# The ConvGLU up-projection of a streaming encoder layer as seven block products instead of eight, from activations that are not yet normalised, with the down products in between

## The chip, the cores and the metric

The kernel runs on one core of a Trainium2 chip. The metric is the device time of one launch in microseconds (us), lower is better. TensorE is called PE here, and its weight loads PEld; VectorE is DVE, ScalarE is ACT, GpSimd is POOL, and SP issues most of the loads.

## The reference

One layer of a hybrid encoder for 640 tokens: 512 of one new stream, and 16 of each of eight running streams. Only the second half of the layer is changed:

```python
h = x + mix @ p['w_o']
hn = rms_norm(h, p['g_ffn'])
up = hn @ p['w_up']                       # 1024 -> 2 x 2816
a, b = jnp.split(up, [D_FF], axis=-1)
c, new_conv = causal_depthwise_conv(a, conv_hist, p['conv_w'], p['conv_b'])   # width 3, by channel
out = h + (jax.nn.gelu(c) * b) @ p['w_down']
```

A final RMS norm follows. All of it is float32.

## The kernel before

**Layout.** Activations lie with features on the 128 partitions and the 640 tokens along the columns: 8 tiles of the model's features, 22 tiles of each half of the up-projection. A matmul takes 128 x 128 weights and 320 tokens (HT). Operands are rounded to a type of fewer bits (F32R), so every operand is two parts, high and low, and every product is three matmuls: high by high, high by low, low by high (mm3, below). A *segment* is the six matmuls of one block of weights over both halves of the tokens; most of the work is written out segment by segment.

```python
120  def mm3(ps, u, b, x, start, stop):
121      hi, lo = (z[:, b * 128:b * 128 + 128] for z in pairs[u])
124      for h in range(2):
125          mm(bank(ps, h)[:, :HT], hi, xh[:, hs[h]], start, False)
126      for h in range(2):
127          mm(bank(ps, h)[:, :HT], hi, xl[:, hs[h]], False, False)
128      for h in range(2):
129          mm(bank(ps, h)[:, :HT], lo, xh[:, hs[h]], False, stop)
155  def slot(u, segs):
156      later(0, lambda: load(u + 3))
157      later(0, lambda: split_hi(u + 1))
158      later(2, lambda: split_lo(u + 1))
```

**Order.** Each engine works through its own instructions strictly in the order in which the program issues them; a tile framework adds the waits. The program keeps a clock of segments: `later(n, fn)` puts a step n segments ahead, and `tick()` issues what is due before each segment's matmuls. Weights come in units of eight blocks (128 x 1024, 512 KB): SP loads unit u + 3 while u is multiplied, ACT rounds unit u + 1 to its high part (L107), and DVE subtracts to get the low part (L112).

**The changed part.** The output projection (eight units, o_evac at L1125) adds the residual, makes the two parts of each normalised tile (times the norm's weights, L170 and L176; the token's 1/rms is applied later, as RS), and sums the squares. Then, for each of the 22 tiles f: one unit gives the gate half (a_evac, L1169 to L1171: PSUM times RS), one the value half (b_evac, L1195); between them DVE runs the convolution (L1179, L1181 twice), ACT the GELU (L1185, L1186), DVE the product (L1198), and ACT and DVE its two parts (L168, L174). POOL copies history and new history (L1168, L1177, L1178). After eight tiles come eight units of down products (L1226 adds each result to h), after eight more the same, and the last six tiles end in the final stage: down products over tokens 0 to 383, then over 384 to 639, with squares (L1249), norm and output (L1265). PARTS = (8, 8, 6) says so.

Of the kernel before, what the change touches and what calls it, by code (L numbers as in the profile page):

```python
# [37 lines left out]
def body(nc, tc, d, ctx):  # L38
# [37 lines left out]
    rst = const.tile([128, 8], F32, name="rst")  # L76
# [19 lines left out]
    res_pool = [None]  # L96

    def split_hi(u):
        if u < N_UNITS:
            if res_pool[0] is not None and u < N_UNITS - 2:  # L100
                hi = res_pool[0].tile([128, 1024], F32R, tag="rh", name=nm("rh"))
                lo = res_pool[0].tile([128, 1024], F32R, tag="rl", name=nm("rl"))
            else:
                hi = wp.tile([128, 1024], F32R, tag="wh", name=nm("wh"))
                lo = wp.tile([128, 1024], F32R, tag="wl", name=nm("wl"))
            pairs[u] = (hi, lo)
            A.activation(hi, raws[u], AF.Copy)  # L107

    def split_lo(u):
        if u < N_UNITS:  # L110
            hi, lo = pairs[u]
            V.tensor_tensor(lo, raws[u], hi.bitcast(F32), op=OP.subtract)  # L112
# [18 lines left out]
    # ---------------------------------------------------------------- events, by segment  # L131
# [8 lines left out]
    def tick():  # L140
        """Start of a segment: what is due, then a piece of the side work."""
# [11 lines left out]
    # one slot per unit: the next unit is split and a later one loaded while this one is multiplied  # L153
# [8 lines left out]
    def split_into(dst, src, scale, d_hi, d_lo):  # L162
        """dst = [hi, lo] of src (times a column), later"""
# [59 lines left out]
    # ---------------------------------------------------------------- side work: S5  # L223
# [7 lines left out]
    def scan_order(t):  # L231
        """(chunk, j) of the prompt and (n, i, j) of the samples in a tile of (j, c) columns"""
# [21 lines left out]
    def paced(ops, budget):  # L254
        """Run (cost, fn) pairs, pausing when the vector engine's share of a segment is used up."""
# [9 lines left out]
    def s5():  # L265
# [62 lines left out]
        # th modulo 2 pi, then sine and 1 - cosine of a quarter of it, doubled twice  # L328
# [33 lines left out]
        # powers 0..8 of lambda-bar  # L362
# [43 lines left out]
        # (lambda-bar - 1) / lambda  # L406
# [17 lines left out]
        def cmul(o_re, o_im, a, b, t, cost):  # L424
            """(o_re, o_im) = a * b, elementwise"""
# [21 lines left out]
        # chunk inputs of the states; the within-chunk response  # L447
# [58 lines left out]
        # C by (part, state) on partitions, [re; im] and [im; re], groups in the order (q, g2, g); in this  # L506
        # order PF of all groups, on both halves of the partitions
# [50 lines left out]
        def stack(q):  # L558
            """The states of eight groups, parts and states on partitions"""
# [66 lines left out]
        # outputs of the chunks  # L626
# [13 lines left out]
    # ---------------------------------------------------------------- side work: attention  # L640
# [36 lines left out]
    def attention():  # L677
# [69 lines left out]
        def prompt_pv(t0, hp, t, ms):  # L747
            # the two heads of a tile in turn: their products lie in two column tiles of the array
# [155 lines left out]
    # ---------------------------------------------------------------- start: norm and the first two units  # L904
# [4 lines left out]
    A.activation(rst, ones[:, 0:8], AF.Sqrt)  # L909
# [91 lines left out]
    # ---------------------------------------------------------------- input projection  # L1001
# [56 lines left out]
    # ---------------------------------------------------------------- GLU, attention's projection, mix  # L1058
# [56 lines left out]
    # ---------------------------------------------------------------- output projection, residual, norm  # L1115
    h_, hn = [], []
    acc2 = mp.tile([128, T], F32, name="acc2", bufs=1)
    xr = {}

    def load_x(i):  # L1120
        if i < 8:
            xr[i] = mp.tile([128, T], F32, tag="xr", name=nm("xr"))
            S.dma_start(xr[i], d["x"][i])

    def o_evac(i, ps):  # L1125
        h = ht()
        V.tensor_tensor(two(h), ps[:, :, :HT], two(xr[i]), op=OP.add)
        load_x(i + 2)
        p = pair()
        split_into(p, h, vcol(C_GF + i), 0, 1)  # L1130
        hn.append(p)
        h_.append(h)
        later(2, lambda: square_h(mp, acc2, h, i == 0))
        if i == 7:
            st = stat_steps(mp, [acc2], RS, 0, 5, ("sS", "sT", "sX"))
            for j, f in enumerate(st):
                later(6 + j, f)
# [3 lines left out]
    later(7, lambda: None)  # L1141

    def o_proj(i):
        ps = bigps()
        slot(U_O + i, [lambda k=k: mm3(ps, U_O + i, k, mixh[k], k == 0, k == 7) for k in range(8)])
        later(0, lambda: o_evac(i, ps))

    for i in range(8):
        o_proj(i)

    # ---------------------------------------------------------------- ConvGLU
    fctx = ExitStack()
# [9 lines left out]
    state = {}  # L1162

    def a_evac(f, ps):
        a = fp[0].tile([128, NA], F32, tag="a", name=nm("a"))
        asm = a[:, 514:NA].rearrange("p (n s) -> p n s", n=NS)
        G.memset(a[:, 0:2], 0.0)  # L1167
        G.tensor_copy(asm[:, :, 0:2], hist[:, f])  # L1168
        V.tensor_tensor(a[:, 2:322], ps[:, 0, :HT], RS[:, 0:320], op=OP.mult)  # L1169
        V.tensor_tensor(a[:, 322:514], ps[:, 1, 0:192], RS[:, 320:512], op=OP.mult)  # L1170
        V.tensor_tensor(asm[:, :, 2:18], ps[:, 1, 192:320].rearrange("p (n i) -> p n i", n=NS),  # L1171
                        RS[:, 512:640].rearrange("p (n i) -> p n i", n=NS), op=OP.mult)
        c = fp[0].tile([128, L], F32, tag="c", name=nm("c"))
# [263 lines left out]
```

## Time and profile before

| | us |
|---|---|
| device time, median of 3 runs (lowest, highest) | 969.23 (967.4, 973.29) |
| span of the profiled execution | 967.0 |
| busy PE, DVE, ACT, POOL in it | 949.5, 543.6, 305.8, 78.2 |

The span runs from the first to the last instruction of the profiled execution; the device time of the runs has besides it what lies before and behind, some 2 us against the median. Busy time counts overlapping matmuls once. DVE is busy in 56% of the span, ACT in 32%, POOL in 8%.

### The profile page before, as it was taken

The page shows a single profiled execution, that of the slowest core. Times are in us where ns is not written, and L with a number is a line of the kernel's source. Part 1 is how long each engine was busy: PE and PEld are TensorE (multiplying, and loading weights), DVE is VectorE, ACT ScalarE, POOL GpSimd, SP SyncE. Part 2 cuts the span into 40 slices and gives each one's busy share as a digit, 9 for nine tenths or more (in the row PEclk, how much of TensorE's full clock was granted, in tenths as well). Part 3 has the DMA queues.
Part 4 walks back from the last instruction along what each step waited for, and adds up shares of the span by engine and source line. Part 5 has one row for each costly group of instructions (what it writes and reads, how often), then busy time and mean ns, then how long its engine had stood idle before and what let it go on. Part 6 is the DMA issues. An engine that isn't in the chain of part 4 may idle for free.

```text
span 967.0 us, 16339 instructions
## 1 busy us (share of the span) xinstructions
PE 949.5 (98%) x6788; PEld 906.3 (94%) x6788; DVE 543.6 (56%) x1033; ACT 305.8 (32%) x497; POOL 78.2 (8%) x157
## 2 busy tenths in 40 slices
PE   8999999999999999999999999999999999999996
PEld 8978999977677899999999999999999999999996
DVE  6884995666565445484555555324555533455545
ACT  7153113434343454433432222111222211122231
POOL 0121303100000000000001101000110100011000
PEclk9999999999999999999999999999999999999998
DMA  6743429764764432223323222222212222222203
GB/s 224 198 150 102 131 83 123 244 191 157 212 184 175 107 101 75 79 93 107 128 66 88 66 87 66 88 66 68 87 66 88 67 87 66 72 82 69 88 28 108
DMA packets 48889, 105.60 MB, mean 109 GB/s; under 512 B 19440, under 2 KB 22704, under 8 KB 48816
## 3 DMA queue, kind: packets, MB, share of 16 engines
q1 hardware_dynamic: 45104, 95.90, 33.0%
q0 software_dynamic: 2848, 7.88, 2.7%
q8 instruction: 53, 0.87, 0.4%
q10 hardware_dynamic: 864, 0.78, 0.2%
q14 instruction: 20, 0.16, 0.1%
HBM read 91.49 MB, written 8.21 MB: 103 GB/s over the span
## 4 chain that ended last, share of the span: by engine, by line
PE 94%; DMA 2%; DVE 2%; ACT 1%; issue 1%; SPq 0%; DVEq 0%; ACTq 0%
PE pb L115 83%; PE sS L115 3%; PE sX L115 2%; DMA qs<-qs 1%; PE sP L115 1%; PE sT L738 1%; PE sX L814 1%; DMA wr<-in_w 1%; PE sS L786 1%; PE sT L802 0%; PE sT L468 0%; DVE ql L668 0%; PE sT L115 0%; DVE h L1265 0%; PE sX L817 0%
## 5 line engine op out<-in xcount | busy, mean ns | idle before, releaser
L115 PE MATMUL pb<-h,wh 128*128 128x320 f32 (+1 forms) x3488 | 665.9, 312 | 1.9 <-ACT h L944 1.0
L115 PEld LDWEIGHTS pb<-h,wh 128*128 128x128 f32 x3488 | 546.1, 188 | 10.5 <-issue 5.2
L115 PE MATMUL pb<-h,wl 128*128 128x320 f32 (+1 forms) x1744 | 400.3, 309 | 0.0
L115 PEld LDWEIGHTS pb<-h,wl 128*128 128x128 f32 x1744 | 292.4, 188 | 0.0
L107 ACT ACTIVATE wh<-wr 128x1024 fp32r<-128x1024 f32 x112 | 118.5, 1058 | 325.2 <-PE pb L115 241.6
L112 DVE TENSOR_TENSOR wl<-wr,wh 128x1024 fp32r<-128x1024 f32 x112 | 136.6, 1220 | 36.7 <-ACT wh L107 36.5
L1226 DVE TENSOR_TENSOR h<-pb,h 128x640 f32<-128x640 f32 x16 | 13.2, 824 | 76.7 <-PE pb L115 76.7
L1169 DVE TENSOR_TENSOR a<-pb,RS 128x320 f32<-128x320 f32 x22 | 10.8, 492 | 77.1 <-PE pb L115 74.9
L1195 DVE TENSOR_TENSOR b<-pb,RS 128x640 f32<-128x640 f32 x22 | 18.1, 825 | 55.4 <-PE pb L115 55.4
L693 ACT ACTIVATE sb<-sb,mx 128x128 f32<-128x128 f32 (+4 forms) x40 | 24.2, 605 | 70.7 <-DVE mx L692 47.2
L1181 DVE SCALAR_TENSOR_TENSOR c<-a,vec,c 128x656 f32<-128x656 f32 x44 | 39.7, 902 | 1.6
L1185 ACT ACTIVATE g<-c 128x512 f32<-128x512 f32 x22 | 13.9, 632 | 83.3 <-DVE c L1181 83.3
L1177 POOL COPY oc<-a 128x2 f32<-128x2 f32 x22 | 4.1, 187 | 371.8 <-DVE a L1170 371.8
L725 DVE CUSTOM_DVE_ANT_0 sb<-sS,pb 128x128 f32<-128x128 f32 (+3 forms) x32 | 15.7, 490 | 24.0 <-PE sS L115 23.8
L115 PE MATMUL pb<-h,rh 128*128 128x384 f32 (+1 forms) x128 | 28.2, 312 | 0.1
L1167 POOL MEMSET a<- 128x2 f32 x22 | 2.1, 96 | 310.7 <-DVE rst L207 310.7
L1046 DVE TENSOR_TENSOR h<-pb,RS 128x640 f32<-128x640 f32 x16 | 13.2, 824 | 19.4 <-PE pb L115 9.9
L1178 POOL COPY oc<-a 128x16 f32<-128x16 f32 x22 | 23.9, 1085 | 0.2
L168 ACT ACTIVATE h<-g 128x640 fp32r<-128x640 f32 x22 | 16.3, 739 | 22.8 <-DVE g L1198 22.8
L115 PEld LDWEIGHTS pb<-h,rh 128*128 128x128 f32 x128 | 21.4, 188 | 0.4 <-DVE h L1240 0.4
L115 PE MATMUL pb<-wh,h 128*128 128x512 f32 x64 | 21.7, 398 | 0.0
L115 PE MATMUL pb<-h,rl 128*128 128x384 f32 (+1 forms) x64 | 19.8, 309 | 0.0
(225 smaller groups left out, 845.0 us busy)
## 6 DMA issues: line engine op xcount, KB each, us to landing
wr<-in_w SPq DMA_DIRECT2D x116, 512.0 KB, 3.6
kc<-in_kc SPq DMA_DIRECT2D x16, 512.0 KB, 6.4
vc<-in_vc SPq DMA_DIRECT2D x16, 512.0 KB, 6.0
xr<-in_x SPq DMA_DIRECT2D x8, 320.0 KB, 2.9
x<-in_x SPq DMA_DIRECT2D x7, 320.0 KB, 6.3
pb<-in_pbias SPq DMA_DIRECT2D x8, 256.0 KB, 6.8
o_y<-h SPq DMA_DIRECT2D x8, 192.0 KB, 1.9
us<-h POOLq DMA_DIRECT2D x4, 320.0 KB, 5.6
```

What stands on the lines that cost most here:

```text
L107: A.activation(hi, raws[u], AF.Copy)
L112: V.tensor_tensor(lo, raws[u], hi.bitcast(F32), op=OP.subtract)
L115: PE.matmul(ps, lhs, rhs, start=start, stop=stop)
L168: A.activation(hi, src, AF.Copy)
L693: A.activation(sb[:, :w], sb[:, :w], AF.Exp, bias=mx[:, 2:3], accum_out=mx[:, 3:4])
L725: V.tensor_tensor_reduce(sb[:, :w], sc[:, :w], pbs[h][:, 512 - w:512], 1.0, -3.0e38, op0=OP.add, op1=OP.max, accum_out=mx[:, 1:2])
L1046: V.tensor_tensor(two(o), ps[:, :, :HT], two(RS), op=OP.mult)
L1178: G.tensor_copy(oc[0][:, f, 2:18].rearrange("p (n s) -> p n s", n=NS), asm[:, :, 16:18])
L1181: V.scalar_tensor_tensor(c, a[:, j:L + j], vcol(C_CW + 3 * f + j), c, op0=OP.mult, op1=OP.add)
L1185: A.activation(g[:, 0:512], c[:, 0:512], AF.Gelu_apprx_tanh)
L1195: V.tensor_tensor(two(b), ps[:, :, :HT], two(RS), op=OP.mult)
L1226: later(0, lambda: V.tensor_tensor(two(h_[i]), ps[:, :, :HT], two(h_[i]), op=OP.add))
```

## The change

The gate and the value block of a tile are taken as one product of 2 x 2 blocks: two blocks of outputs, two halves of the 1024 inner features (k 0 to 3 and 4 to 7), two halves of the tokens. It is computed with seven block products (Strassen's scheme in Winograd's form), each of four k by three matmuls:

```diff
-PARTS = (8, 8, 6)
+PARTS = (2, 4, 4, 4, 4, 4)
...
+    def parts_far(pool, tags, key, src, width):
+        hi, lo = (pool.tile([128, width], F32R, tag=t, name=nm(t)) for t in tags)
+        n = src.shape[-1]
+        A.activation(lo[:, 0:n], src, AF.Copy, scale=-1.0)
+        A.activation(hi[:, 0:n], src, AF.Copy)
+        G.dma_start(lo[:, 0:n], src, accum_op=OP.add)
...
+    def parts_near(pool, tags, key, src, width):
...
+        A.activation(hi[:, 0:n], src, AF.Copy)
+        V.tensor_tensor(lo[:, 0:n], src, hi[:, 0:n].bitcast(F32), op=OP.subtract)
...
+    def weight_sums(f):
...
+        V.tensor_tensor(s1, a21, a22, op=OP.add)
+        V.tensor_tensor(s2, s1, a11, op=OP.add)
+        V.tensor_tensor(s3, a11, a21, op=OP.add)
+        V.tensor_tensor(s4, s2, a12, op=OP.add)
...
+    PRODUCTS = (("A11", "B11", "sS"), ("s1", "t1", "sP"), ("s2", "t2", "sT"), ("A12", "B21", "sS"),
+                ("s3", "t3", "sX"), ("A22", "t4", "sT"), ("s4", "B22", "sP"))
...
+    def gate(f):
+
         G.tensor_copy(asm[:, :, 0:2], hist[:, f])
...
+        V.tensor_tensor(u3, b_("sT"), u3, op=OP.subtract)
+        V.tensor_tensor(a_t[:, 2:514], g_t[:, 0:512], RS[:, 0:512], op=OP.mult)
...
+            at(q - 24, lambda f=f, u=R1: load_raw(("1", f), u))
+            at(q - 17, lambda f=f, u=R2: load_raw(("2", f), u))
...
+            at(q + 2, lambda: A.activation(u2, b_("sS"), AF.Copy))
+            at(q + 8, lambda: V.tensor_tensor(b_t[:, lo_], b_("sS"), u2, op=OP.add))
+            at(q + 8, lambda: V.tensor_tensor(u2, b_("sT"), u2, op=OP.add))
+            at(q + 10, lambda: V.tensor_tensor(u3, b_("sX"), u2, op=OP.add))
...
+            at(q + 10, lambda: V.tensor_tensor(u2, b_("sP"), u2, op=OP.add))
+            at(q + 12, lambda f=f: gate(f))
...
+                at(q - 7, lambda f=f, u=u, cols=cols: load_raw(("d", f), u, cols))
+                at(q + 3, lambda f=f: parts_far(wp, W8, ("d", f), R["d", f], 1024))
...
+        pr = pos - 12 if n < 5 else max(pos - 12, items[n - 5][0] + 2)
+        if w == "s1":
+            at(pr - 2, lambda f=f: weight_sums(f))
+        far = parts_near if w == "A22" else parts_far
...
+        at((5, 6, 8, 9)[j], fn)
...
+        at(11 + 2 * i, lambda i=i: V.tensor_tensor(h_[i], h_[i], RM, op=OP.mult))
```

- A product takes two segments, written at q, q + 2, ... of a tile that starts at segment q; a tile takes 14. Its result lies in one of four single PSUM banks (sS, sP, sT, sX), of which three are used twice within a tile. DVE and one ACT copy (u2) put the seven results together: gate in g_t and a_t, value in b_t.
- The token's 1/rms is applied once, to the gate (RS). The value and the residual stay larger by the token's rms: h is multiplied by it (RM, L1415), and the final norm (fin_stat) takes it out.
- The activation sums t1 to t4 are made once, by pairs of tiles k and k + 4 (sums, L1173), during the output projection, whose units stand in the order 0, 4, 1, 5, 2, 6, 3, 7.
- Per tile, DVE adds weights (s1 to s4, 128 x 512 each). High and low parts are made per product, in rings of five buffers (wf): for six of the seven by two ACT copies and an adding DMA from POOL (parts_far), for A22 by ACT and DVE (parts_near). Raw weights, two units for each tile and one for its down products (d), share three buffers (wr).
- Down products stand behind each tile's 14 segments: none in tiles 0 and 1, 4 segments in tiles 2 to 5, 8 in tiles 6 to 21 (so tiles of 14, 18 and 22 segments), over the two or four tiles of the part before. Each h gets five additions (L1358) where it got two. The last four tiles' down products are the final stage, 32 segments of three matmuls for each range of tokens, where it was 48.

On PE, the end of a tile's gate unit and the start of its value unit before (pb: PSUM, h: the parts of the activations, wh and wl: the parts of the weights; x2 are the two halves of the tokens):

```order
L115 MATMUL pb860_6063<-h763_5180,wh856_6006 128x320 x2
L115 MATMUL pb860_6063<-h764_5181,wh856_6006 128x320 x2
L115 MATMUL pb860_6063<-h763_5180,wl857_6007 128x320 x2
L115 MATMUL pb867_6133<-h703_4724,wh864_6073 128x320 x2
L115 MATMUL pb867_6133<-h704_4725,wh864_6073 128x320 x2
L115 MATMUL pb867_6133<-h703_4724,wl865_6074 128x320 x2
```

The end of the first product and the start of the second now (fh and fl: the parts of a block of weights or of a sum):

```order
L115 MATMUL sS806_5295<-h799_5281,fh775_5158 128x320 x2
L115 MATMUL sS806_5295<-h799_5281,fl776_5159 128x320
L115 MATMUL sP809_5318<-h720_4826,fh782_5185 128x320
L115 MATMUL sP809_5318<-h721_4827,fh782_5185 128x320
L115 MATMUL sP809_5318<-h720_4826,fl783_5186 128x320
L115 MATMUL sP809_5318<-h745_4975,fh782_5185 128x320
L115 MATMUL sP809_5318<-h746_4976,fh782_5185 128x320
L115 MATMUL sP809_5318<-h745_4975,fl783_5186 128x320
```

A row that stood for both halves of the tokens stands for one; x2 in the first rows is the high and the low part of the activations, which lie in one tile there.

On DVE, one tile in mid-stage before, from the gate's evacuation on:

```order
L1169 TENSOR_TENSOR a791_5404<-pb783_5341,RS_78 128x320
L1170 TENSOR_TENSOR a791_5404<-pb783_5341,RS_78 128x192
L1171 TENSOR_TENSOR a791_5404<-pb783_5341,RS_78 128x8x16
L112 TENSOR_TENSOR wl795_5414<-wr779_5279,wh794_5413 128x1024
L1179 TENSOR_SCALAR c792_5410<-a791_5404,vec_76 128x656
L1181 SCALAR_TENSOR_TENSOR c792_5410<-a791_5404,vec_76,c792_5410 128x656 x2
L1195 TENSOR_TENSOR b798_5474<-pb790_5403,RS_78 128x640
L1198 TENSOR_TENSOR g796_5458<-g796_5458,b798_5474 128x640
L112 TENSOR_TENSOR wl801_5479<-wr785_5344,wh800_5478 128x1024
L174 TENSOR_TENSOR h789_5402<-g796_5458,h788_5401 128x640
```

Around the products of tile 3 now: the low part of A22 of tile 3, the weight sums of tile 4, and the combinations of tile 3 with its gate:

```order
L1270 TENSOR_TENSOR fl904_5872<-wr866_5660,fh903_5871 128x512
L1280 TENSOR_TENSOR s913_5916<-wr902_5862 128x512
L1281 TENSOR_TENSOR s914_5917<-s913_5916,wr891_5789 128x512
L1282 TENSOR_TENSOR s915_5918<-wr891_5789,wr902_5862 128x512
L1283 TENSOR_TENSOR s916_5919<-s914_5917,wr891_5789 128x512
L1374 TENSOR_TENSOR b_t_4666<-sS917_5924,u2_4667 128x320
L1375 TENSOR_TENSOR u2_4667<-sT910_5898,u2_4667 128x320
L1376 TENSOR_TENSOR g_t_4665<-sX920_5944,u2_4667 128x320
L1377 SCALAR_TENSOR_TENSOR g_t_4665<-sP905_5875,g_t_4665 128x320
L1379 TENSOR_TENSOR u2_4667<-sP905_5875,u2_4667 128x320
L1311 TENSOR_TENSOR g_t_4665<-sT923_5965,g_t_4665 128x320
L1312 TENSOR_TENSOR a_t_4663<-g_t_4665,RS_78 128x512
```

The two low parts of 1024 columns have gone; four weight sums of the next tile stand between the low part of A22 and the combinations that empty sS and sT. SP loads wr902 (the second unit of tile 4) into the buffer of wr866, so behind the first of these rows.

On POOL, two tiles before (a: the gate with its history, oc: the new history):

```order
L1167 MEMSET a805_5536 128x2
L1168 COPY a805_5536<-hist_77 128x8x2
L1177 COPY oc_5249<-a805_5536 128x2
L1178 COPY oc_5249<-a805_5536 128x16
L1167 MEMSET a819_5668 128x2
L1168 COPY a819_5668<-hist_77 128x8x2
```

One tile of 22 segments now (the adding DMAs):

```order
L1310 COPY a_t_4663<-hist_77 128x8x2
L1263 DMA fl1159_7434<-s1153_7408 128x512
L1318 COPY oc_4669<-a_t_4663 128x2
L1319 COPY oc_4669<-a_t_4663 128x16
L1263 DMA fl1162_7457<-s1154_7409 128x512
L1263 DMA fl1166_7480<-wr1138_7301 128x512
L1263 DMA fl1170_7503<-s1155_7410 128x512
L1263 DMA wl1178_7561<-wr1164_7469 128x1024
L1263 DMA fl1180_7572<-s1156_7411 128x512
```

Between the same copies stand seven adding DMAs, six of 128 x 512 and one of 128 x 1024.

## Rows read from the trace of the kernel before

**Rows 1.** Stages of 100 us: busy time of the engines, granted clock, DMA share, GB/s.

```profile
550.00:650.00 100.00, 100.00 (x684) 100.00 (x683) 43.91 (x56) 21.13 (x26) 7.39 (x16) 1.00 0.24 79
750.00:850.00 100.00, 100.00 (x684) 100.00 (x683) 41.22 (x53) 20.54 (x24) 5.93 (x14) 1.00 0.24 74
```

**Rows 2.** The chain that ended last: start us, us, what, with its count.

```profile
332.60 160.16 PE pb L115 x1092
...
492.75 1.01 PE sS L115 x10
...
495.63 0.89 PE sT L115 x8
496.74 421.19 PE pb L115 x2865
918.57 20.57 PE pb L115 x120
...
942.57 14.31 PE pb L115 x120
```

**Rows 3.** DVE by shape from 500 us on: count, busy us, mean ns, idle before.

```profile
L112 DVE TENSOR_TENSOR wl<-wr,wh 128x1024 fp32r<-128x1024 f32 x59 | 71.9, 1219 | 0.4 <-ACT wh L107 0.4
L1181 DVE SCALAR_TENSOR_TENSOR c<-a,vec,c 128x656 f32<-128x656 f32 x44 | 39.7, 902 | 1.6
L1198 DVE TENSOR_TENSOR g<-g,b 128x640 f32<-128x640 f32 x22 | 18.2, 825 | 2.6 <-DVE b L1195 0.5
...
L1179 DVE TENSOR_SCALAR c<-a,vec 128x656 f32<-128x656 f32 x22 | 13.5, 613 | 0.0
...
L1169 DVE TENSOR_TENSOR a<-pb,RS 128x320 f32<-128x320 f32 x21 | 10.3, 492 | 74.9 <-PE pb L115 74.9
...
L1265 DVE SCALAR_TENSOR_TENSOR h<-h,vec,RS 128x384 f32<-128x384 f32 x8 | 4.7, 613 | 1.3 <-ACT RS L218 1.3
...
L1240 DVE TENSOR_TENSOR h<-pb,h 128x256 f32<-128x256 f32 x8 | 3.4, 421 | 1.5 <-PE pb L115 1.3
```

**Rows 4.** Timeline around 511 us, PE then DVE: start us, us, instruction, idle before.

```profile
510.66 0.60 PE L115 MATMUL pb<-h,wh 128*128 128x320 f32 x3
```
```profile
510.86 0.49 DVE L1169 TENSOR_TENSOR a<-pb,RS 128x320 f32<-128x320 f32 x1 [3.42 <-PE pb L115]
511.27 0.35 DVE L1170 TENSOR_TENSOR a<-pb,RS 128x192 f32<-128x192 f32 x1
```

**Rows 5.** Timeline of DVE at 941 us, each step needing the one before.

```profile
940.79 0.17 DVE L204 RECIPROCAL rst<-sr 128x3 f32<-128x3 f32 x1
940.99 0.16 DVE L205 TENSOR_TENSOR sr<-rst 128x3 f32<-128x3 f32 x1
```

**Rows 6.** The chain near its end: DVE releases PE.

```profile
959.71 0.17 DVE rst L207
959.88 0.14 issue
960.02 0.70 PE sT L115 x4
```

**Rows 7.** ACT by shape from 480 us on, columns as in rows 3.

```profile
L107 ACT ACTIVATE wh<-wr 128x1024 fp32r<-128x1024 f32 x62 | 65.7, 1060 | 217.3 <-PE pb L115 179.7 <-issue 37.6
L168 ACT ACTIVATE h<-g 128x640 fp32r<-128x640 f32 x22 | 16.3, 739 | 22.8 <-DVE g L1198 22.8
L1185 ACT ACTIVATE g<-c 128x512 f32<-128x512 f32 x22 | 13.9, 632 | 83.3 <-DVE c L1181 83.3
L1186 ACT ACTIVATE g<-c 128x128 f32<-128x128 f32 x22 | 6.5, 293 | 0.0
...
L1185 ACT ACT_TABLE_LOAD x1 | 1.3, 1283 | 3.8 <-issue 3.8
```

**Rows 8.** DMA issues: count, size of each, median us from issue to landing.

```profile
wr<-in_w SPq DMA_DIRECT2D x116, 512.0 KB, 3.6
...
o_v<-h POOLq DMA_DIRECT2D x5, 256.0 KB, 2.6
```

**Rows 9.** Ten us each in the attention stage, columns as in rows 1.

```profile
280.00:290.00 10.00, 8.11 (x57) 6.17 (x56) 6.21 (x20) 3.61 (x9) 0.00 (x0) 0.93 1.02 262
290.00:300.00 10.00, 10.00 (x99) 8.30 (x97) 3.86 (x16) 2.29 (x6) 0.00 (x0) 0.90 0.31 121
```

More of the change, by code (lines that the diff above doesn't have):

```diff
@@ L91, in load @@
     def load(u):
-        if u < N_UNITS:
+        if u < U_F:
             raws[u] = wp.tile([128, 1024], F32, tag="wr", bufs=3, name=nm("wr"))
             S.dma_start(raws[u], d["w"][u])
-    res_pool = [None]
     def split_hi(u):
[L99 to L105, printed above, removed]
+        if u < U_F:
+            hi = wp.tile([128, 1024], F32R, tag="wh", name=nm("wh"))
+            lo = wp.tile([128, 1024], F32R, tag="wl", name=nm("wl"))
             pairs[u] = (hi, lo)
@@ new lines, in body, with load_x, mid, sq @@
+    RM = fp.tile([128, T], F32, name="RM")
+    oc = fp.tile([128, KF, 18], F32, name="oc")
+    asm = a_t[:, 514:NA].rearrange("p (n s) -> p n s", n=NS)
+    lo_, hi_ = slice(0, HT), slice(HT, T)
+    u3 = g_t[:, lo_]
+    def load_x(j):
+        if j < 8:
+            i = O_ORDER[j]
+            xr[i] = ht()
+            S.dma_start(xr[i], d["x"][i])
+    def mid():
+        return h2.tile([128, T], F32, tag="m", name=nm("m"), bufs=4)
+    def sq(i):
+        if i == 0:
+            A.activation(RM, h_[i], AF.Square)
+        else:
+            q = ht()
+            A.activation(q, h_[i], AF.Square)
+            V.tensor_tensor(RM, RM, q, op=OP.add)
@@ L1139, in body, with o_evac, o_proj @@
+    def o_evac(j, ps):
+        i = O_ORDER[j]
+        h = h2.tile([128, T], F32, tag="h", name=nm("h"), bufs=8)
+        V.tensor_tensor(two(h), ps[:, :, :HT], two(xr[i]), op=OP.add)
+        load_x(j + 2)
+        h_[i] = h
+        if i >= 4:
+            later(1 if j < 7 else 0, lambda: sums(i - 4))
+        later(3, lambda: sq(i))
     load_x(0)
     load_x(1)
-    later(7, lambda: None)
-    def o_proj(i):
+    def o_proj(j):
         ps = bigps()
-        slot(U_O + i, [lambda k=k: mm3(ps, U_O + i, k, mixh[k], k == 0, k == 7) for k in range(8)])
-        later(0, lambda: o_evac(i, ps))
@@ L1158, in c_sample, with at, load_raw @@
+    c0 = clock[0] + 64
+    segs = []
+    def at(pos, fn):
+        events.setdefault(c0 + pos, []).append(fn)
     def c_sample(c):
         return bass.AP(tensor=c.tensor, offset=c.offset + 514, ap=[c.ap[0], [18, NS], [1, TS]])
[L1162 to L1167, printed above, removed]
+    R = {}
+    ops = {}
+    held = {}
+    def load_raw(key, u, cols=slice(0, 1024)):
+        n = cols.stop - cols.start
+        R[key] = wp.tile([128, 1024], F32, tag="wr", bufs=3, name=nm("wr"))[:, 0:n]
+        S.dma_start(R[key], d["w"][u, :, cols])
@@ new lines, in gelu, with product @@
+    def gelu():
+        A.activation(g_t[:, 0:512], c_t[:, 0:512], AF.Gelu_apprx_tanh)
+        A.activation(g_t[:, 512:640].rearrange("p (n i) -> p n i", n=NS), c_sample(c_t), AF.Gelu_apprx_tanh)
+    cs = {}
+    def product(f, j):
+        if j < 3:
+            cs[f] = (ht(F32R), ht(F32R))
+        else:
+            cs[f] = tuple(h2.tile([128, T], F32R, tag="m", name=nm("m"), bufs=4) for _ in range(2))
+        V.tensor_tensor(g_t, g_t, b_t, op=OP.mult)
+        A.activation(cs[f][0], g_t, AF.Copy)
@@ L1206, in body, with down_evac @@
+    def down_evac(i):
+        V.tensor_tensor(two(h_[i]), downs[i][:, :, :HT], two(h_[i]), op=OP.add)
+    items = []
+    f0, prev = 0, None
+    for p, nf in enumerate(PARTS):
         for j in range(nf):
             f = f0 + j
-            if fp[0] is None:
-                def open_fp():
-                    mctx.close()
-                    fp[0] = fctx.enter_context(tc.tile_pool(name="ffn", bufs=2))
-                    oc[0] = fp[0].tile([128, KF, 18], F32, name="oc", bufs=1)
-                later(7, open_fp)
@@ L1214, in body @@
-            proj(u, hn, lambda ps, f=f: a_evac(f, ps))
-            p = pair()
-            cs.append(p)
-            if part == 2 and j == nf - 1:
-                res_pool[0] = fctx.enter_context(tc.tile_pool(name="res", bufs=4))
-            proj(u + 1, hn, lambda ps, f=f, p=p: b_evac(f, ps, p))
-            u += 2
-        f0 += nf
-        if part < 2:
-            def down(i, u, cs):
-                ps = bigps()
-                slot(u, [lambda k=k: mm3(ps, u, k, cs[k], k == 0, k == 7) for k in range(8)])
-                later(0, lambda: V.tensor_tensor(two(h_[i]), ps[:, :, :HT], two(h_[i]), op=OP.add))
-            for i in range(8):
-                down(i, u + i, cs)
-            u += 8
+            q = len(segs)
@@ new lines, in body @@
+            at(q + 14, lambda: V.tensor_tensor(b_t[:, hi_], b_("sP"), u2, op=OP.add))
+            at(q + 16, gelu)
+            at(q + 17, lambda f=f, j=j: product(f, j))
+            at(q + 18, lambda f=f: product_lo(f))
+            if prev is not None:
+                pf, pn = prev
+                per = 8 // nf
+                w = per * pn * 128
+                u = U_D[p - 1] + (j * w) // 1024
+                cols = slice((j * w) % 1024, (j * w) % 1024 + w)
+                at(q - 7, lambda f=f, u=u, cols=cols: load_raw(("d", f), u, cols))
+                at(q + 3, lambda f=f: parts_far(wp, W8, ("d", f), R["d", f], 1024))
+                for o in range(per):
+                    i = j * per + o
+                    for k in range(pn):
+                        segs.append(lambda i=i, f=f, o=o, k=k, pn=pn, pf=pf: down_seg(i, ("d", f), o, k, pn, pf + k))
+                    at(len(segs), lambda i=i: down_evac(i))
@@ L1232, in body @@
+    for j in range(8):
+        o_proj(j)
+    for sfn in segs:
+        tick()
+        sfn()
     segs = ((0, SEG_A), (SEG_A, T))
@@ L1234, in body @@
     last = [ht(), ht()]
-    rs3 = [None]
     def fin_evac(sg, i, ps):
```

280 lines of the change are left out of this document (196 added, 84 removed).

## The prediction

> **What bounds the kernel now.** I read the stages first: in two stretches of 100 us in the middle of the changed part PE is busy all the time at the full clock (2.4 GHz), DVE about 42%, ACT 21%, and the DMA engines a quarter [rows 1]. Then the chain of waits: from 332.6 us on it is PE alone, in runs of 1092 and 2865 matmuls with only statistics between them [rows 2]. So a matmul that goes is time that goes, as long as nothing else comes up to PE. The price of one: 160.16 us / 1092 and 421.19 / 2865 both give 0.147 us for 320 columns [rows 2]; a segment of six is 0.88 us. The short tail runs give 20.57 / 120 = 0.171 for 384 columns and 14.31 / 120 = 0.119 for 256 [rows 2].
>
> **What it removes.** A tile of the up-projection was two units of eight blocks by six matmuls, 96; seven products of four k by three matmuls are 84. The down products keep their matmuls: only their order and the split into parts change. 22 x 12 x 0.147 us = **38.7 us** off PE. DVE also loses two low parts of 1024 columns per tile, at 1.22 us each [rows 3].
>
> **Prices for what it adds.** DVE on SBUF or PSUM: 640 columns 0.825, 1024 1.22, 320 from PSUM 0.49, and 0.90 for a scalar-tensor step of 656 [rows 3]; between them 512 columns come to 0.69 and a scalar-tensor step of 320 to 0.53 (384 take 0.61). ACT: 1.06 for 1024, 0.74 for 640, 0.63 for 512 [rows 7], so 0.46 for 320. DVE starts 0.20 us after the PE work it needs has ended [rows 4], a dependent DVE step loses 0.03 [rows 5], and PE starts 0.14 after DVE [rows 6].
>
> **A tile in the steady state** (the sixteen of 22 segments, 19.4 us of PE). DVE has four weight sums 2.8, one low part 0.69, seven combinations 3.5, gate 1.0, convolution 0.61 + 2 x 0.90 = 2.4, product and its low part 1.65, two additions to h 1.65: 13.7 of 19.4 us. ACT has six pairs of copies of 512 (7.6), one of 1024 (2.1) less the near one's missing half (0.6), u2 0.5, GELU 0.9 and the product's high part 0.74: about 11. POOL only issues. None is full. The tightest PSUM return is sP: it is filled by s1's product at segment 4, read twice by DVE after segment 10 and overwritten at segment 12. The chain 0.20 + 0.49 (u3) + 0.53 (g_hi) + 0.41 to 0.49 (u2) + 0.14 is 1.8 against two segments, 1.76: about 0.1 us a tile, **+1.6**.
>
> **The start of the changed part.** The first products need the activation sums, and those of the last pair begin only when the last output block is evacuated: evacuation 0.20 + 0.82, ACT's B2 0.74, three dependent DVE steps of 0.5, the parts of B1: about 4.0 us until the last block of the first product can run. PE can do 9 of the first 12 matmuls meanwhile (1.3 us), so 2.6 are lost. Then PE's own order holds the two broadcasts of the norm at segments 8 and 9, and DVE has the four weight sums of the second tile (2.8) ahead of the six small norm steps (0.2 each): they end some 1.9 us after PE wants them. The second broadcast is five matmuls of 128 columns, 0.11 each by 0.89 / 8 [rows 2]: 0.6. **+5.1**.
>
> **The second tile.** sT is written twice a tile, and PE may write A22's product only when DVE has read s2's (L1375). Between that point in the first tile and in the second, DVE has 17.1 us of work: combinations 2.0, gate 1.5, convolution 2.4, b_hi and b_lo 1.0, near low 0.69, product and low 1.65, weight sums 2.8, u2 0.5, and six multiplications of h by RM at 0.83. On top it waits about 2.4, since the near part's high copy is queued on ACT behind the GELU, whose first call loads a table of 1.28 us [rows 7]. 19.5 against PE's 14 segments, 12.3: **+7.2**.
>
> **The third tile** has two more RM multiplications and the same wait for ACT, and from it on the weight buffer counts: SP loads the second unit of tile f+1 into the buffer that the near part of A22 of tile f reads last, and in the tiles of 14 and 18 segments DVE has the weight sums of f+1 ahead of the combinations of f (the rows of DVE shown for the change). Near low part until 10.2 us after the last release, load 3.6 [rows 8], sums 2.8, b_lo and u2 1.0: 17.8 with a hand-over, against 12.3. That counts the whole load as exposed; I take **+5.0**.
>
> **Tiles four to six** (18 segments). At segment 2 of a tile, 1.76 us, ACT does u2 (0.46) and A22's high part (0.63), DVE its low part until 4.0; the load lands at 7.6, the sums end at 10.4, u2 at 11.4; PE wanted sT at segment 10, 8.8 us. 2.65 late each, **+8.0**. If the load landed 2.7 us sooner this would be nothing; nothing in the trace shows it sooner. From the seventh tile on the sums come behind the combinations, and this goes.
>
> **The end.** The final stage has 32 segments of three for each range of tokens, where it was 48. Over the last range PE has 96 x 0.119 = 11.4 us, and DVE eight outputs of 384 columns at 0.61 [rows 3], eight additions of 256 at 0.42 [rows 3], seven additions of squares at about 0.42 and some nine small steps: 12.7. **+1.3**.
>
> **The clock.** In the attention stage PE is idle for 1.9 us of 10, and the granted clock of that stretch and the next is 0.93 and 0.90 [rows 9]: part of each went at 1.2 GHz in place of 2.4, and 0.7 + 1.0 = 1.7 us of full-speed work were lost. The idle stretches above are as long; I count one such loss, **+1.7** (none would be 0, one for each of six 10).
>
> **Adding DMAs.** A tile of 22 segments has six of 256 KB and one of 512 KB. No adding DMA stands in the trace. Plain ones do: POOL's 256 KB land in 2.6 us [rows 8], and a share of 0.24 for 79 GB/s [rows 1] makes 329 GB/s for all 16 engines, so 0.8 us of all of them for 256 KB, 1.6 for 512. Let x be what an adding byte takes of the engines against a plain one. The tightest of them is s4: ACT ends its low part about 5.5 us into the tile; ahead of it in POOL's queue is the 512 KB of the down weights; PE wants it at 10.9. It lands at 5.5 + 1.8 (2.6 less its own 0.8) + 0.8 (half of a load of SP in between) + x (1.6 + 0.8) = 8.1 + 2.4 x. At x = 1 that is 10.5: hidden, nothing to pay. At 1.5 it is 0.8 late, at 2 it is 2.0 late, in sixteen tiles. All loads and adding DMAs of a tile take 4.8 + 6.4 x of its 19.4 us, so the engines are full only at 2.3. A gain is excluded, since an adding DMA moves no fewer bytes; I take x = 1, the nearest row, and keep 2 as the other end.
>
> **Sum.** 967.0 (span) - 38.7 + 5.1 + 7.2 + 5.0 + 8.0 + 1.6 + 1.3 + 1.7 = 958.2; the device time is 2.2 above the span (969.2 against 967.0), so **960 us**. Of 38.7 us saved 30 go back, 25 of them in the first six tiles.
>
> **Rivals.**
> A, the forecast: 960, chance 0.38, within 952 to 968 as the single waits come out.
> B, adding DMAs somewhat dearer, x near 1.5: 16 x 0.8 = 13 more, **973**, chance 0.18. For it: a queue that serves SP's loads and POOL's at once; against it: 14.4 of 19.4 us of the engines.
> C, adding DMAs at the price of two transfers, x = 2: PE waits at the first low-part matmul of s4 in each of sixteen tiles, 2.0 x 16 = 32 more, **992, slower than before**. It decides from x = 1.7, where 16 x 2.4 x (1.7 - 1.17) = 20 us take the rest of the gain. For it: each adding DMA reads source and destination both; against it: nothing in this trace. Chance 0.22.
> The Trainium skill, "Collectives: The Full Stack", in "The bandwidth ceiling: the fold count and why AG ≠ RS ≠ AR", says that a transfer that adds is slower because it needs two source reads, not because of the arithmetic, with 62.28 against 32.35 GB/s between cores. By that page x would be 1.9 and the time 988; no run here shows it yet, and it is the rule that speaks most against this change.
> D, the early waits mostly don't occur, because loads land sooner or DVE gets through its queue sooner than summed: without tiles two to six, 960 - 20 = **940**. For it: the terms add waits end to end, and each of them has slack that I can't see; against it: the order on DVE is fixed, and the sums stand ahead of the releases there. Chance 0.22.
>
> **Range and chances.** The single waits spread A by 8 us to either side. From 938 to 992 about 2 in 10 is left out: half of C above, a part of D below. The runs of this kernel spread over 6 us, so 1% (9.7 us) is about what a measurement can tell from no change. Faster than 959.5: D and half of A, 0.41; within 1%: half of A and most of B, 0.33; slower than 979: C and a little of B, 0.26.
>
> **What would show it.** 1848 matmuls of the up-projection; DVE busy around 70% and ACT around 55% in the late tiles. Right as to the early waits: PE idle at the first write of sT for A22 in tiles two to six, waiting for DVE's L1375, with DVE idle ahead of it at L1280 for wr, and none of that after the seventh tile; the clock below 1 once or more there. Right as to x: the adding DMAs (L1263) land in 2.6 to 4 us and no matmul waits for fl. C shows as PE idle at the matmuls with fl of s4 in every tile of 22 segments, with landing times of 5 us and more. Most of all the forecast fails if ACT or DVE run late in the steady tiles, where each 0.6 us is 10 us in the sum: I have bounds for each queue there, but not for their coupling.

## The result and the profile after

The changed kernel takes 1006.25 us (median; 1003.98 to 1007.23) against 968.61 us before: the ratio is 1.037, with a 95% interval of 1.034 to 1.040. It is **slower by 3.7%**, beyond the upper end of the range. The profiled execution has a span of 1002.2 us, 35.2 more than before, though 38.7 us of matmuls are gone.

The same two stretches as in rows 1, with the busy time of PE, its weight loads, DVE, ACT and POOL, the granted clock, the DMA share and GB/s:

```profile
550.00:650.00 100.00, 87.88 (x556) 86.53 (x555) 60.30 (x99) 49.53 (x90) 30.96 (x45) 0.93 0.74 158
750.00:850.00 100.00, 93.89 (x620) 92.22 (x619) 60.27 (x101) 49.30 (x88) 31.66 (x48) 0.98 0.80 176
```

Before, PE was busy all the time there, at the full clock [rows 1]. Now it idles for 12 and 6 us of 100, its clock is below 1, and the DMA engines go from a quarter to three quarters and more. What PE waits for from 480 us on (us in total, times, longest; the first eight of eleven rows):

```profile
PE sT L115 <- DVE u L1375: 21.0, 5, 5.0
PE sP L115 <- DMA fl<-s: 20.3, 14, 2.2
PE pb L115 <- DVE rst L1223: 2.0, 1, 2.0
PE pb L115 <- DVE h L1445: 1.8, 3, 0.6
PE sX L115 <- DVE rst L1488: 1.6, 1, 1.6
PE sS L115 <- DVE h L1170: 1.1, 1, 1.1
PE sP L115 <- DVE b_t L1383: 1.0, 1, 1.0
PE sS L115 <- ACT h L1169: 0.9, 1, 0.9
```

The first row is the wait of A22's product for DVE in the second to sixth tile, one each: 4.21, 4.98, 3.43, 3.37 and 5.04 us. The second is s4's product waiting for its low part in 14 of the sixteen tiles of 22 segments. The others are the start of the changed part, one wait at sP in the second tile, and the end.

One such wait at s4, PE's timeline (start, us, instruction, idle before), and the clock around it in pieces of 4 us:

```profile
798.03 0.53 PE L115 MATMUL sP<-h,fh 128*128 128x320 f32 x2
800.77 0.42 PE L115 MATMUL sP<-h,fl 128*128 128x320 f32 x1 [2.21 <-DMA fl<-s]
...
802.43 1.27 PE L115 MATMUL pb<-h,wh 128*128 128x320 f32 x4
```
```profile
796.00:800.00 4.00, 2.56 (x17) 2.23 (x16) 3.27 (x6) 1.77 (x4) 1.58 (x3) 1.00 1.08 211
800.00:804.00 4.00, 3.23 (x16) 3.23 (x17) 2.90 (x6) 0.75 (x2) 1.25 (x4) 0.78 1.01 243
804.00:808.00 4.00, 4.00 (x24) 4.00 (x24) 2.65 (x4) 2.14 (x5) 0.86 (x2) 0.80 0.43 75
808.00:812.00 4.00, 4.00 (x29) 4.00 (x29) 2.38 (x3) 1.41 (x3) 1.25 (x2) 1.00 0.76 130
```

PE has s4's high part and stands 2.21 us for the low one. Then its clock drops: four matmuls take 1.27 us where they take 0.75 at the full clock, and 24 matmuls go into 4 us where 29 go later. So a wait can cost more than its length. That tile, from the first matmul of one to that of the next (787.47 to 810.91), took 23.44 us, against 19.43 for one with no wait: 2.21 of waiting, about 0.3 of restart (what the other tiles with a wait and no drop of the clock take besides it), and 1.5 of clock.

POOL in the same tile:

```profile
787.58 0.87 POOL L1263 DMA_DIRECT2D fl<-s  x1 [0.80 <-ACT fl L1261]
791.63 0.87 POOL L1263 DMA_DIRECT2D wl<-wr  x1 [3.18 <-ACT wl L1261]
793.09 0.87 POOL L1263 DMA_DIRECT2D fl<-s  x1 [0.60 <-ACT fl L1261]
796.10 0.87 POOL L1263 DMA_DIRECT2D fl<-wr  x1 [2.14 <-ACT fl L1261]
```

The 512 KB of the down weights (wl) go out at 791.63, and s4's 256 KB at 793.09, 5.6 us into the tile; PE can go on at 800.77, 7.7 us later. The most frequent DMA issues (KB each, median us to landing) from 480 us on:

```profile
wr<-in_w SPq DMA_DIRECT2D x62, 512.0 KB, 4.4
fl<-s POOLq DMA_DIRECT2D x88, 256.0 KB, 4.2
fl<-wr POOLq DMA_DIRECT2D x48, 256.0 KB, 4.0
wl<-wr POOLq DMA_DIRECT2D x18, 512.0 KB, 7.0
```

Plain transfers took 3.6 us for SP's 512 KB and 2.6 for POOL's 256 KB [rows 8]; these have become slower.

And DVE around the fifth tile's wait:

```profile
577.62 0.69 DVE L1270 TENSOR_TENSOR fl<-wr,fh 128x512 fp32r<-128x512 f32 x1
582.64 0.69 DVE L1280 TENSOR_TENSOR s<-wr 128x512 f32<-128x512 f32 x1 [4.32 <-DMA wr<-in_w]
583.36 0.69 DVE L1281 TENSOR_TENSOR s<-s,wr 128x512 f32<-128x512 f32 x1
583.97 0.68 DVE L1282 TENSOR_TENSOR s<-wr,wr 128x512 f32<-128x512 f32 x1
585.24 0.69 DVE L1283 TENSOR_TENSOR s<-s,wr 128x512 f32<-128x512 f32 x1 [0.58 <-DMA fl<-s]
585.85 0.48 DVE L1374 TENSOR_TENSOR b_t<-sS,u 128x320 f32<-128x320 f32 x1
586.36 0.49 DVE L1375 TENSOR_TENSOR u<-sT,u 128x320 f32<-128x320 f32 x1
```

DVE reads the buffer of the old weights for the last time (L1270), stands idle 4.32 us until the new ones have landed in it (L1280), does the sums, and only then the two steps that empty sS and sT (L1374, L1375), which had long been due. A second wait in these rows was not in the forecast: L1283 writes s4 of the next tile over the buffer from which s4's adding DMA of this tile still reads.

### The profile page after: what moved, and what is told of

Its sections match the earlier page's. It is cut to its first block, busy times and chain, and to the rows that moved or that the text cites. A ratio compares the mean times of both kernels' runs of the same rounds, so it can differ in the third digit from the quotient of the medians.

```text
span 1002.2 us, 16841 instructions
## 1 busy us (share of the span) xinstructions
PE 936.8 (93%) x6534; PEld 884.4 (88%) x6534; DVE 625.3 (62%) x1249; ACT 450.1 (45%) x809; POOL 190.9 (19%) x294
## 4 chain that ended last, share of the span: by engine, by line
PE 59%; DMA 13%; issue 11%; DVE 8%; ACT 4%; POOL 4%; SPq 0%; DVEq 0%; POOLq 0%; ACTq 0%
PE pb L115 40%; DMA fl<-s 11%; PE sS L115 6%; PE sP L115 4%; PE sT L115 3%; POOL fl L1263 3%; PE sX L115 2%; DMA qs<-qs 1%; PE sT L738 1%; POOL wl L1263 1%; DVE s L1283 1%; PE sX L814 1%; DVE h L1464 1%; ACT fl L1261 1%; ACT wl L1261 1%
## 5 line engine op out<-in xcount | busy, mean ns | idle before, releaser
L115 PE MATMUL pb<-h,wh 128*128 128x320 f32 (+2 forms) x2000 | 389.8, 316 | 2.9 <-DVE h L1445 1.2
L115 PEld LDWEIGHTS pb<-h,wh 128*128 128x128 f32 x2000 | 315.0, 190 | 12.1 <-issue 5.2
L115 PE MATMUL pb<-h,wl 128*128 128x320 f32 (+2 forms) x1000 | 231.1, 311 | 0.0
L115 PEld LDWEIGHTS pb<-h,wl 128*128 128x128 f32 x1000 | 169.3, 190 | 0.0
L115 PE MATMUL sT<-h,fh 128*128 128x320 f32 x352 | 84.1, 327 | 21.0 <-DVE u L1375 21.0
L1263 POOL DMA_DIRECT2D fl<-s x88 | 77.0, 880 | 128.1 <-ACT fl L1261 112.8
L107 ACT ACTIVATE wh<-wr 128x1024 fp32r<-128x1024 f32 x50 | 52.8, 1056 | 101.2 <-PE pb L115 86.9
L115 PE MATMUL sP<-h,fh 128*128 128x320 f32 x352 | 83.2, 323 | 1.0 <-DVE b_t L1383 1.0
L112 DVE TENSOR_TENSOR wl<-wr,wh 128x1024 fp32r<-128x1024 f32 x50 | 61.0, 1220 | 36.1 <-ACT wh L107 36.0
L115 PE MATMUL sS<-h,fh 128*128 128x320 f32 x352 | 78.5, 310 | 2.0 <-DVE h L1170 1.1
L115 PE MATMUL sP<-h,fl 128*128 128x320 f32 x176 | 57.8, 328 | 20.4 <-DMA fl<-s 20.3
```

Of the source, the lines that this page charges most:

```text
L115: PE.matmul(ps, lhs, rhs, start=start, stop=stop)
L1263: G.dma_start(lo[:, 0:n], src, accum_op=OP.add)
```

## The experiments

All of them change the changed kernel, with 1006.25 us; the kernel before is at 969 to 970 us beside them. The theory, from this profile: an adding DMA takes nearly twice a plain one's share of the DMA engines, which makes s4 late in the late tiles; DVE, in order behind the load of the next weights, makes sT late in the early ones; PE's idle stretches cost clock besides. The rival for the late tiles: ACT or POOL come to s4 too late, whatever the DMAs cost. The rival for the early ones: DVE has too much to do.

**Plain DMAs in place of adding ones.**

```diff
-        G.dma_start(lo[:, 0:n], src, accum_op=OP.add)
+        G.dma_start(lo[:, 0:n], src)
```

> All adding DMAs become plain ones of the same size (the low parts are then the values themselves, so that part of the computation is changed). Theory: a byte of an adding DMA takes about 1.7 times the DMA engines' time of a plain one (49.7% against 22.3% of the engines for 46.2 against 35.7 MB), and that is what makes s4 late. Then the 256 KB land in about 3 us in place of 4.2, PE's waits for fl at sP (20.3 us) go, with the 0.3 us of restart behind each and the three drops of the clock that follow them: 1006 - 20 - 5 - 5 = about 977. The early waits at sT (21 us) stay. Rival: s4 is late because ACT or POOL get to it late (POOL is occupied 0.88 us by each issue): then the waits stay, and the time is above 1000.

It took 974.62 us (what this kernel computes is no longer the layer; only its time counts here). The waits for fl fell from 20.3 us to 2.5. Those at sT, which were expected to stay, fell from 21.0 to 15.7: about a quarter of them hung on the adding DMAs too. The queues from 640 to 900 us (q0 is POOL's, q1 SP's; packets, MB, share of the 16 engines' time), first with adding DMAs, then with plain ones:

```profile
q0 software_dynamic: 12321, 25.57, 54.5%
q1 hardware_dynamic: 5360, 19.53, 24.9%
...
fl<-s POOLq DMA_DIRECT2D x50, 256.0 KB, 4.2
```
```profile
q0 software_dynamic: 13433, 28.14, 33.2%
q1 hardware_dynamic: 5718, 20.80, 27.7%
...
fl<-s POOLq DMA_DIRECT2D x53, 256.0 KB, 2.6
```

54.5% of 260 us for 25.57 MB is 5.54 us of all engines per MB, against 33.2% for 28.14 MB, 3.07: **x, the price of an adding byte against a plain one, is 1.81**. The plain price is the one taken from rows 1 (329 GB/s, 3.04 us per MB), and 2.6 us to landing is that of rows 8. ACT's and POOL's instructions are the same in both kernels, so the rival falls.

**s4's parts near.**

```diff
-        far = parts_near if w == "A22" else parts_far
+        far = parts_near if w in ("A22", "s4") else parts_far
```

> s4's low part comes from ACT and DVE (parts_near) in place of ACT and an adding DMA. Theory: s4 is the one part that is late, as the last in POOL's queue behind the 512 KB of the down weights; all others have slack. The waits for fl go and nothing takes their place: about 976 to 980. Rival: the next adding DMA, or DVE with 0.69 us more a tile in front of its combinations, is late in s4's place: above 995.

It took 971.34 us, 5 below what was expected. No wait for fl is left: of the first fifteen tiles of 22 segments fourteen take 19.42 to 19.44 us each, and one 20.56, with a wait of 0.66 for the down weights. sT's waits fell too, to 16.4 us: no L1283 waits for a DMA any more. So s4 was the one late part. This run alone doesn't tell whether its place in the queue or the adding DMAs that are saved made the difference; the next one does.

**The down weights' parts two segments later**, so that on ACT and in POOL's queue s4 goes first.

```diff
-                at(q + 3, lambda f=f: parts_far(wp, W8, ("d", f), R["d", f], 1024))
+                at(q + 5, lambda f=f: parts_far(wp, W8, ("d", f), R["d", f], 1024))
```

> The parts of the down weights are made two segments later, so that the 512 KB adding DMA stands behind s4's in POOL's queue, not ahead. Theory: s4 is late because its 256 KB wait for those 512 KB on the same DMA engines, at 1.7 times a plain byte: it lands some 2.7 us sooner, and PE's waits for fl at sP go. The down weights then land at about 13.5 us of the tile where PE wants them at 12.9, so 0.5 to 1 us a tile shows there: about 985. Rival: the order doesn't matter, s4 is late by its own ACT copies: 1000 or more.

It took 968.08 us, 17 below what was expected, and level with the kernel before (ratio 0.999, 0.997 to 1.001), at the same number of bytes. One wait for fl is left, 1.1 us, and no matmul waits for the down weights. POOL in one tile of this run, which starts at 783.98:

```profile
788.63 0.87 POOL L1263 DMA_DIRECT2D fl<-s  x1 [2.63 <-ACT fl L1261]
790.10 0.87 POOL L1263 DMA_DIRECT2D wl<-wr  x1 [0.60 <-ACT wl L1261]
```

s4's DMA goes out at 4.6 us of the tile, 1.0 sooner, and has no 512 KB in front. The fear for the down weights was too high: they go out at 6.1 and, with a median landing time of 6.5 us, come just in time. This order also lowers the waits at sT, to 13.8 us.

**The weight sums behind the combinations** in the third to sixth tile.

```diff
-            at(pr - 2, lambda f=f: weight_sums(f))
+            sp = pr - 2 if not 3 <= f <= 6 else pos - 2 - 18 + 11
+            at(sp, lambda f=f: weight_sums(f))
+        if w != "A11":
+            pr = max(pr, sp)
```

> The weight sums of the fourth to seventh tile stand behind the combinations of the tile before on DVE, as they do from the eighth on. Theory: the waits at sT in the third to sixth tile (16.8 us) come from DVE waiting in order for the weights, which wait for a buffer; they go, with the clock that they cost (some 8 us): about 983, a little of the third tile's wait staying since DVE is full there. Rival: DVE has simply too much to do in these tiles, or s1 and its parts come late now: 1000 or more.

It took 988.79 us, 6 above what was expected. PE's waits now:

```profile
PE sP L115 <- DMA fl<-s: 23.4, 18, 2.9
PE sT L115 <- DVE u L1375: 4.2, 1, 4.2
```

sT's waits fell from 21.0 to 4.2 us, which is the second tile's alone; the third to sixth take 16.99, 16.23, 16.81 and 16.74 us, against 23.59, 21.04, 20.97 and 23.30. DVE does the same work there, so the order was the cause. The waits for fl rose by 3.1 us, to 18 in number; they begin in the third tile now, and five drops of the clock lie behind such waits from the seventh tile on, where there were two.

**PE kept busy during the wait.**

```diff
+                if w == "s3" and 1 <= f <= 5:
+                    one = segs[-1]
+                    def more(f=f, n=n, one=one):
+                        one()
+                        for _ in range(NFILL):
+                            up_seg2(f, n)
+                    segs[-1] = more
```

Here up_seg2 is both halves of the product in one step, and NFILL is 2.

> In the second to sixth tile PE does the product of s3 three times over in the same bank (each time from the start, so the result is the same), 24 more matmuls of 0.147 us = 3.5 us each, just ahead of the wait at sT of 3.4 to 5 us. Theory: the clock falls because PE stands idle there; PE then idles 0 to 1.5 us, the drops to half clock behind these waits (2.6, 2.8, 1.7, 1.7 and 2.4 us) mostly don't occur, and the time falls by about 8 to 10 us although PE has 17.6 us more to do: about 997. Rival: the clock falls for another reason (the load on the whole chip), or the drops cost nothing since the waits are set by DVE: 1006 or more.

It took 998.83 us, 7.4 below the changed kernel with 120 matmuls (17.6 us) more. Two stretches of the changed kernel, and the same of this one:

```profile
520.00:560.00 40.00, 30.82 (x177) 30.59 (x177) 25.29 (x42) 19.61 (x38) 13.71 (x20) 0.83 0.67 136
560.00:600.00 40.00, 33.20 (x204) 32.73 (x203) 25.68 (x42) 19.00 (x36) 12.62 (x19) 0.91 0.72 152
```
```profile
520.00:560.00 40.00, 36.41 (x244) 35.47 (x244) 29.12 (x48) 22.10 (x41) 13.85 (x21) 1.00 0.71 147
560.00:600.00 40.00, 39.30 (x266) 38.83 (x266) 25.57 (x42) 20.78 (x38) 13.84 (x21) 1.00 0.77 159
```

With most of PE's idle time filled, the clock stays at its full level. The second to sixth tile together take 100.8 us in place of 109.1: the matmuls that were added went into time that was lost anyway. DVE's and the DMAs' work is the same, so it was PE's idling that took the clock.

**Both cures together** (s4 near, sums behind).

> s4's parts near, and the weight sums behind the combinations, together. Theory: the two causes lie in different stretches of time (the third to sixth tile, and the tiles of 22 segments), so their gains add: 971 less some 18 = about 953. Rival: the adding DMAs are close to late in every part once the early waits are gone (in the run with the sums alone the waits for fl began in the third tile already), so other parts come late: above 962.

It took 956.16 us, ratio 0.985 (0.982 to 0.989): **faster than the kernel before by 1.5%**. The gains nearly add: 34.9 and 17.5 us alone, 50.1 together.

**The multiplications by RM later**, alone and with both.

```diff
-        at(11 + 2 * i, lambda i=i: V.tensor_tensor(h_[i], h_[i], RM, op=OP.mult))
+        at(38 + 18 * (i // 2) + 2 * (i % 2), lambda i=i: V.tensor_tensor(h_[i], h_[i], RM, op=OP.mult))
```

> Only the multiplications by RM moved. Theory: the second tile's wait falls from 4.2 us to nearly none with its clock loss, the third's by up to 1.6: about 998. But the third to sixth tile get 1.65 us more of DVE's work each behind the release, which should cost nothing. Rival: no change, 1004 to 1007.

It took 1006.04 us: nothing gained, the rival's number. The second tile's waits did fall, from 5.2 to 3.6 us, but with the multiplications gone, DVE there stands idle 1.53 us at L1283, for s4's adding DMA. In the two profiles the gain is lost again in the first tile, 1.6 us longer, and behind a third drop of the clock in the late ones.

> The same, and the eight multiplications of h by RM spread over the third to sixth tile in place of the first and second. Theory: the second tile's waits (4.2 us at sT, 1.0 at sP, and 2.6 of the clock) come from DVE's queue, of which six multiplications are 5 us: most of it goes, some 6 us below the run without it, about 947. Rival: the table load of the GELU and the near part behind it set that wait: no gain beyond 1 us.

It took 955.05 us, 1.1 below the run without, where 6 to 9 were expected. With s4 near no DMA holds L1283: the second tile goes from 20.50 us to 15.39. But the third to seventh are 0.2 to 1.3 us longer each, in part at sP (L1383, 0.7 to 1.1 us): DVE now has two low parts and up to two multiplications in each.

**The multiplications on POOL**, with both cures, and then with the later down weights too.

```diff
-        at(11 + 2 * i, lambda i=i: V.tensor_tensor(h_[i], h_[i], RM, op=OP.mult))
+        at(11 + 3 * i, lambda i=i: G.tensor_tensor(h_[i], h_[i], RM, op=OP.mult))
```

> s4 near, the sums behind the combinations, and the eight multiplications by RM on POOL in place of DVE, in the first to third tile. Theory: moved within DVE, the multiplications only made other tiles late (waits at sP of 0.7 to 1.1 us in the fourth to seventh); on POOL, which has time, the second tile's wait goes and nothing comes in its place: about 950. Rival: POOL's multiplications stand in front of its adding DMAs, which come late in the first tiles: 956 or more.

> The same, with the parts of the down weights two segments later. Theory: with s4 off the DMA queue its place there is free, and the later down weights only come nearer to their own deadline: 0 to 3 us slower than the run without. Rival: the order matters for other parts too: faster.

They took 967.17 and 958.77 us: the theory misses in both. No matmul waits for fl, so the first rival's cause is not it either. The wait moved to sP, which waits for DVE: 5.1 us in the second tile of both runs, and 6.2 and 7.7 in the third. DVE and then POOL of the first of these runs, at the end of the first tile:

```profile
508.92 1.59 DVE L1312 TENSOR_TENSOR a_t<-g_t,RS 128x512 f32<-128x512 f32 x1
510.44 0.28 DVE L1313 TENSOR_TENSOR a_t<-g_t,RS 128x128 f32<-128x128 f32 x1
510.83 0.62 DVE L1320 TENSOR_SCALAR c_t<-a_t,vec 128x656 f32<-128x656 f32 x1
511.48 4.95 DVE L1322 SCALAR_TENSOR_TENSOR c_t<-a_t,vec,c_t 128x656 f32<-128x656 f32 x1
```
```profile
508.05 1.90 POOL L1418 TENSOR_TENSOR h<-h,RM 128x640 f32<-128x640 f32 x1
...
511.84 3.88 POOL L1418 TENSOR_TENSOR h<-h,RM 128x640 f32<-128x640 f32 x2
```

While POOL multiplies, a convolution step of 0.90 us takes 4.95, and the gate's of 0.69 takes 1.59. The run with the later down weights is the faster one, as its rival had it, and no tile of it from the fourth on has a wait. Between the two profiled executions, which are 5.2 us apart, that is worth 3.4 from the seventh tile on; 2.3 lie ahead of the first tile, where the two kernels are the same. The medians are 8.4 apart, and the two profiles don't show where the rest lies.

**The two orders alone**, with all parts but A22's far.

> All six parts far as in the changed kernel, only the two orders changed: the parts of the down weights two segments later, and the weight sums behind the combinations. Theory: the order alone cures both (the run with the later down weights has no wait for fl in 20 of 21 tiles at the same bytes), so about 968 - 13 = 955. Rival: without the early waits the adding DMAs of the third to sixth tile are late, as in the run with the sums alone: above 960.

It took 955.79 us, ratio 0.986 (0.982 to 0.989), as expected: no engine gets other work, and the changed kernel becomes 50 us faster and **1.5% faster than the kernel before**. The rows for the two stretches:

```profile
550.00:650.00 100.00, 98.70 (x659) 96.43 (x659) 71.40 (x121) 58.07 (x106) 39.52 (x57) 1.00 0.90 195
750.00:850.00 100.00, 100.00 (x680) 99.43 (x679) 65.20 (x108) 54.74 (x97) 33.69 (x51) 1.00 0.87 191
```

The DMA engines are at 0.87 to 0.90 here, above the 0.74 and 0.80 of the slow kernel: a high share by itself doesn't make PE wait. At the same price of a byte, which transfer stands before which decides.

**The two orders, and the multiplications by RM later on DVE.**

> The two orders (down weights' parts two segments later, sums behind the combinations), all parts far but A22's, and the multiplications by RM on DVE in the third to sixth tile. Theory: with s4 far DVE has room in those tiles, and with the down weights later s4's adding DMA no longer holds up the fourth weight sum, so the second tile's waits (4.2 and 1.0 us and the clock behind them) go for the most part and little comes in their place: about 951. Rival: as in the run with s4 near, the third to seventh tile lose at sP what the second gains: 954 to 957.

It took 959.21 us (0.990; 0.988 to 0.993), above even the rival's numbers: the second tile's wait at sT only fell to 3.5 us, with 1.53 at L1283 again, and the fourth to seventh wait 0.7 to 0.9 us each for fl. Why the multiplications on DVE make those parts late was not tried.

## Why the prediction was wrong

- **What goes** was right: a tile without a wait takes 19.43 us for 22 segments, 0.883 each, where 0.88 was forecast.
- **Adding DMAs, "I take x = 1, the nearest row"**: this step failed, and it is the largest miss. x is 1.81. Put into the prediction's own sum, s4 lands at 8.1 + 2.4 x 1.81 = 12.4 us, 1.5 late; measured were 14 waits of 1.45 on the mean: the sum was right, the price in it wrong. 20.3 us of waiting and some 0.3 of restart behind each make about 25 us that the forecast put at nothing. The place, the mechanism and the price were those of rival C (x = 2, 32 us), which had 0.22. The ratio that the prediction took from the Trainium skill, "Collectives: The Full Stack", in "The bandwidth ceiling: the fold count and why AG ≠ RS ≠ AR", fits: its 62.28 against 32.35 GB/s is 1.93, the runs here show 1.81 between adding and plain DMAs within the core. That the second read is the reason is not shown by any run here. The prediction had found nothing in the trace against x = 2 and an argument for it, the two reads; x = 1 had only the nearest row behind it, one of plain transfers.
- **The clock, "I count one such loss, +1.7"**: this failed too. The second to sixth tile took 33.4 us more than their segments; 22.0 of these are the waits, some 2 the restarts, so 9 to 10 are the clock, and the run with PE kept busy bears this out, with 8.3 us less for these five tiles. Two later tiles lost 1.5 each. So about 12 to 13 us in place of 1.7. The prediction had the row for it and the bound, 10; it counted one loss, though its own sum had five waits as long as that of rows 9.
- **The early waits** were nearly right in sum, 22.0 against 20.2: second tile 5.2 (7.2 forecast), third 4.98 (5.0), fourth to sixth 11.8 (8.0). That the sum came so near is partly luck, since single terms miss both ways. In the last three the load took longer than 3.6 us among the adding DMAs (4.3, 4.2 and 5.75), and s4's DMA held up L1283 for 0.5 to 0.6 us each (in two of the three the profile names ACT as what ended that wait, but s4's DMA landed 0.1 us before each); in the third it held it up for 1.86, which the forecast's 5.0 did not hold. In the second tile the reason is half wrong: DVE's queue with six multiplications was full, but behind it stood the wait at L1283, as moving them showed. The prediction's list of DVE's work there also adds up to 17.5 us, not 17.1.
- **The first tile** was about right: waits of 0.88, 1.09, 0.44 and 1.96, 4.4 us, and the second broadcast of 1.0, against 5.1. With the restarts behind the waits it took 6.7 more: 21.1 us, of which 12.3 are segments and 2.1 statistics that stood there before.
- **The steady tiles, "+1.6"**: no wait at sP there; 0.07 us a tile, 1.1 in sum.
- **The end, "+1.3"**, was too small. From the end of the first range of tokens to the end of the span it took 28.1 us before (938.98 to 967.04) and takes 26.5 now (975.65 to 1002.18), though 48 matmuls of 0.119, 5.7 us, have gone: 4.2 more. Three waits of 0.6 for DVE at pb are the crowding that was forecast; the rest wasn't tried.
- **Ahead of the changed part** lie 1.4 of the 35.2 us, in stages that the change doesn't touch: matmul 3550 of the trace, in the output projection, starts at 485.8 us in place of 484.4. In the profiled executions of the experiments it starts between 484.5 and 488.5, so a difference of a few us between two profiles needs a look at where it lies.
- **The range** left out what happened, because C was priced with the clock of A: the dearer adding DMAs and the clock that goes with the early waits belong in one case. With x = 1.81 and the clock, the prediction's own terms give 960 + 25 + 11, or 996. The rest is the sizes of the first six tiles and of the end, and the 1.4 us ahead of them.

## What to carry to other kernels

Price an adding DMA within SBUF at about 1.8 plain ones until a run says otherwise, and then look at which transfer stands in front of the one with the least slack: moving one 512 KB transfer in each tile, with the copies that prepare it, behind it was worth 38 us here. When a sum forecasts idle stretches of the engine that bounds the kernel, put the loss of clock behind each of them into the same case. In an engine that works in order, nothing that waits for a load belongs in front of what releases another engine.

## What the runs showed of the hardware

- An adding DMA (SBUF to SBUF, 2 KB per partition) took 1.81 times the engines' time of a plain one, and a median of 4.2 us to landing against 2.6 for 256 KB, among this kernel's other transfers.
- A multiplication of 128 x 640 took 1.8 to 2.9 us on POOL against 0.82 on DVE. Beside two of them in a row, a DVE step with two operands in SBUF took 4.95 us for 0.90 (and beside one, another took 1.59 for 0.69).
- With each of PE's five idle stretches of 3.4 to 5.0 us at sT the clock went to 1.2 GHz, in the idle stretch itself or soon behind it; of the 14 of 0.6 to 2.2 us at s4 only two were followed by 1.2 GHz, the ones of 1.92 and 2.21 us.
